# A two-level Strassen matmul with GELU: one more split product, two lent result buffers, and 21 buffer cells chosen anew

## The chip, the cores and the metric

The kernel runs on one core of a Trainium2 chip. The metric is device time in microseconds (us) of one execution. TensorE (PE) multiplies, VectorE (DVE), ScalarE (ACT) and GpSimd (POOL) work on tiles, and SyncE (SP) and POOL issue the transfers: here POOL fetches and SP stores.

## The reference

Two float32 matrices of 4096 x 4096 are multiplied, and the tanh form of GELU is applied to the product:

```python
def reference(a, b):
    x = np.matmul(a, b)
    return 0.5 * x * (1 + np.tanh(np.sqrt(2 / np.pi) * (x + 0.044715 * x**3)))
```

## The kernel before

**Two levels of Strassen.** A, B and C are cut into quadrants of 2048 x 2048 (called "11", "12", "21", "22"). Instead of eight products of quadrants the kernel computes seven, P1 to P7, of sums of quadrants (the Winograd form: P1 is A11 x B11, P2 A12 x B21, and P3 to P7 use sums on one or both sides), and adds them up into the four quadrants of C. Operands are 16-bit floats, sums of products are 32-bit.

The work is tiled by **groups**: a group is one block of 512 rows and 512 columns in each of the four quadrants of C, so there are 4 x 4 = 16 groups. One product of a group is 512 x 2048 x 512: four row tiles (i = 0 to 3) by 16 steps of 128 x 512 columns, 64 matmuls, over four banks of PSUM (`acc`). Such a product can itself be **split**: seven smaller products of half its size instead of eight. Done on one group (`split`, `stage`, `part_pe` at L1011; its matmuls are L1026), it takes 14 parts of eight matmuls of 256 columns; its operands are sums of A blocks and B blocks made by VectorE (`combine2`, L941), its parts are added in PSUM by VectorE (`add_part`, L1044) and copied by ScalarE (L1040).

The groups come in three kinds:

- group 0 (`first_group`), before anything is in place;
- groups 1 to 5 (`raw_group`), which work from the matrices themselves in the order P1, P2, P5, P6, P7, P4, P3, with unsplit matmuls at L581. The table `RAW_CUT` says which of their products are split. A split P7 runs in turns with P4; a split P3 runs in turns with P4 too, or, where P7 is split as well, is handed to the next group and runs in turns with its P1 (`pending`);
- groups 6 to 15 in five pairs of neighbouring column blocks (`late_pair`): (6,7), (8,9), and so on. Here a product is split over both blocks at once (`split_pair`), with matmuls of full 512 columns (L1853), 14 parts of eight: `ORDER = "10 11 70 71 20 21 60 61 50 51 30 31 40 41"`, the first digit is the small product and the second its row tile. B operands come back from DRAM in quarters (`k_unit`, one per product and column block, fetched at L822), and running sums are parked there (`park`).

In `split_pair` the operands are made in place as soon as the parts that read the old contents have been issued:

```python
                if once("T1", "1", "7"):
                    sums["5"] = inner_sum(1, as_inner(sums["6"]), x11, sums.get("7"))
...
                    make("12", "22", "11")
                if once("T4", "1", "2"):
                    make("21", "21", "11")
```

T1's two steps make what part 5 multiplies (a sum of A blocks, then one of B blocks of 128 x 4096), T4 makes part 4's B operand over the block that parts 20 and 21 read. Behind part 7 ScalarE copies its bank out (`copy_bank`, L1862); behind parts 1 and 6 it copies a bank into another (`copy_over`, L1865), which a later part then adds to.

**Results.** A finished bank is added by VectorE to a small buffer (`add_bank`, L1299) or from a buffer into a bank (`into_bank`, L1304), goes through GELU on ScalarE (L1277, or straight from PSUM) and is stored by SP (L822). Result buffers are called `y` in the profile and are 128 x 512 floats; they come out of the list `free_small`. Beside it, VectorE adds up squares of B (L1384), which a check of the value range uses.

**Cells.** Everything else in SBUF lies in 28 cells of 128 x 2048 16-bit values (`bR_73` to `bR_80`, `aD_81` to `aD_84`, `stage_85` and `stage_86`, each of which holds two). `free_cells` is the list of free ones; `new_cell` takes its first, `new_unit` and `new_chunk` neighbours of it. A cell taken early is one whose former readers have to be through before it may be written.

**Who sets the order.** The program is first built as a list of operations with what each reads and writes (`Plan.add`). `Plan.schedule` then walks through planned time: TensorE's operations keep their order, and each other engine takes, among those ready, the one that is due first. Durations and transfers are planned with fixed costs. So another cell or buffer changes what an operation must wait for, hence its planned start, hence the order written for VectorE, ScalarE, POOL and SP, in places far behind as well. The engines run that order as written.

Of the kernel before, what the change touches and what calls it, by code (L numbers as in the profile page):

```python
# [91 lines left out]
    return {name: mode for mode, names in kw.items() for name in names.split()}  # L92


N_RAW = 6
RAW_MAKES = {}
RAW_CUT = {1: "P3", 2: "P7 P3", 3: "P3", 4: "P3", 5: "P7"}
GROUPS = {
    6: modes_of(m="P1 P2 P3 P4 P5 P6 P7"),
    7: modes_of(m="P1 P2 P3 P4 P5 P6 P7"),  # L100
# [14 lines left out]
TURN_PLAN = (("11", "11", "P1", None), ("21", "12", "S4", None), ("12", "S1", "P5", None), ("22", "S2", "next", "P1"))  # L115
BEHIND = 2
FRONT = 2
LEND = ()
SQUARES_3 = ("12",)
NEAR = 2  # L120
CASTS = {4: ((1, 'P3'), (2, 'P3')), (8, 'P5'): ((0, 'P2'),)}
# [225 lines left out]
def half_path(  # L347
# [379 lines left out]
    for n, whats in (  # L727
# [20 lines left out]
        for what in whats.split():  # L748
# [11 lines left out]
            for h in (0, 1) if half else (None,):  # L760
# [9 lines left out]
                else:  # L770
                    pairs = [({"A": load_a, "B": load_b}[x], xs) for x, xs in args]
# [34 lines left out]
    free_cells, free_small = [], [x for x in (8, 9, 0, 1, 2, 3, 10, 11, 12, 13, 14) if x not in SPARE]  # L806
# [18 lines left out]
    def c(x):  # L825
        return ("c", x)

    def new_cell():
        return free_cells.pop(0)

    def new_unit():
        got = []
        for _ in range(2):
            pairs = [k for k, x in enumerate(free_cells) if x ^ 1 in free_cells[:k]]
            x = free_cells[pairs[0]] & ~1
            free_cells.remove(x)
            free_cells.remove(x + 1)
            got += [x, x + 1]
        return got

    def new_chunk():
        x = min((k for k in free_cells if k ^ 1 in free_cells), key=lambda k: max(map(free_cells.index, (k, k ^ 1)))) & ~1
        free_cells.remove(x)
        free_cells.remove(x + 1)
        return x
# [3 lines left out]
    def new_small(lend=False):  # L849
        own = [f for f in free_small if f in lent]  # L850
        if lend and own:
            free_small.remove(own[0])
            return own[0]
        if not free_small or lend and len(free_cells) > 1:
            x = new_cell()
            for h in range(2):
                f = len(small)
                small.append(cell(x)[:, h * W : (h + 1) * W].bitcast(F32))
                plan.alias["f", f] = ("c", x, h)
                free_small.append(f)  # L860
            lent[f], lent[f - 1] = (x, f - 1), (x, f)
            if lend:
                return free_small.pop()
        return free_small.pop(0)
# [57 lines left out]
    def a_quarter(src, q):  # L922
        if src[0] == "raw":
            t = a_phys[src[1], q // 2].rearrange("p x y -> p (x y)")
            return t[:, (q % 2) * CELL : (q % 2 + 1) * CELL], [("a", src[1], q // 2, h) for h in (0, 1)]
        x = src[1][q]
        return cell(x), [c(x)]
# [59 lines left out]
    def unsplit(*args):  # L987
        run(quarters(*args))

    def run(*lists):  # L990
        for row in zip(*lists):
            for fn in row:
                fn()
# [115 lines left out]
    def stages_of(z, done=None, ready=None):  # L1109
        z.ready = ready  # L1110

        def one(k):
            stage(z, k)
            if k == 4 and done and not ready:
                for i in range(RT):
                    done(i)

        return [lambda k=k: one(k) for k in (1, 2, 3, 4)]
# [16 lines left out]
    def made_here(unit_cells, release=lambda p: None, ends=lambda: None):  # L1135

        def quarter(kw):
            k, w = int(kw[0]) - 1, int(kw[1]) - 1
            x = unit_cells[2 * k]
            return wide_of(x)[:, :, w * HC : (w + 1) * HC], [("c", x, w), ("c", x + 1, w)]  # L1140

        def prepare(k):
            if k == 1:
                combine2(*quarter("11"), quarter("12"), quarter("11"), -1)
            elif k == 2:
                combine2(*quarter("11"), quarter("22"), quarter("11"), -1)
                combine2(*quarter("12"), quarter("22"), quarter("12"), -1)
            elif k == 3:
                combine2(*quarter("21"), quarter("21"), quarter("11"), -1)
                ends()  # L1150

        at = {"1": "11", "2": "21", "3": "22", "4": "21", "5": "11", "6": "11", "7": "12"}

        def of(p):
            t, toks = quarter(at[p])
            if p == "1":
                toks = toks + quarter("12")[1]
            full = wide_of(unit_cells[2 * (int(at[p][0]) - 1)])

            def rhs(j, wide):  # L1160
                return full[:, j, :] if wide else t[:, j, :]

            return rhs, toks, (lambda: release(p))

        return of, prepare
# [109 lines left out]
    def out_of(gi, i, ih, jh, f):  # L1275
        t = sm(f)
        act("gelu", lambda: nc.scalar.activation(t, t, ACT.Gelu_apprx_tanh), [("f", f)], [("f", f)])  # L1277
        store_out(gi, i, ih, jh, f)
# [17 lines left out]
    def add_bank(f, s, i, g=None):  # L1296

        g = f if g is None else g
        dve("add", lambda: nc.vector.tensor_tensor(out=sm(g), in0=bank(s, i), in1=sm(f), op=ALU.add),  # L1299
            [("f", f)], [("f", g), ("p", s, i)])  # L1300
        return g
# [110 lines left out]
    def raw(quad):  # L1412
        return ("raw", slots["a"][quad])

    def blk(cells):
        return ("blk", cells)

    def slot_cells(slot):
        return tuple(slot * 4 + q for q in range(QPH))
# [67 lines left out]
    def raw_group(gi, keep_units, makes, fetch=(), next_nb=None, turn=None, pending=None):  # L1487

        cut = RAW_CUT.get(gi, "").split()

        mb, nb = groups[gi]
        X, Y = 0, 1
        sl = dict(slots["b"])
        s11, s12, s21, s22 = (slot_cells(sl[x]) for x in ("11", "12", "21", "22"))
# [33 lines left out]
        if turn:  # L1528
            s2, s3 = SA, blk(SB)
        else:  # L1530
            s2, s3 = SB, raw("21")
# [84 lines left out]
        def load_next(quad, old):  # L1616
            if next_nb is not None:
                load_raw(next_nb, quad, sl[old])

        def here(cells):  # L1620
            return made_here(cells)

        def p4(s, fresh, done):
            return quarters(s, lambda q: a_quarter(raw("22"), q), lambda q: s21[q], fresh, done)
# [9 lines left out]
        def p7_out(i):  # L1634
            add_bank(u[i], X, i)
            out_of(gi, i, 1, 0, u[i])
            f = new_small(i in LEND)
            add_bank(v[i], X, i, f)
            out_of(gi, i, 1, 1, f)

        def p4_ends():
            if turn:
                turn_quad(turn, "22", raw("22"), (24, 26))
            if next_nb is None and gi + 1 in REFETCH:
                for q in range(QPH):
                    fetch_unit_to(nb, "P2", q, s21[q])
# [5 lines left out]
        if "P7" in cut:  # L1652
            def p4_add(i):
                add_bank(u[i], Y, i)

            if "P4" in cut:
                fourth = stages_of(split(Y, raw("22"), here(s21), True), p4_add)
            else:
                fourth = p4(Y, True, p4_add)
            if "P4" in cut:  # L1660
                run(fourth)
                run(stages_of(split(X, s3, here(s12), True), p7_out))
            else:
                run(fourth, stages_of(split(X, s3, here(s12), True), p7_out))
            load_next("21", "12")
            load_next("12", "21")
            p4_ends()
            if "P3" in cut:
                later_ = third, after
            else:  # L1670
                unsplit(Y, lambda q: a_quarter(blk(s2), q), lambda q: s22[q], True, c12)
                after()
        else:
            unsplit(X, lambda q: a_quarter(s3, q), lambda q: s12[q], False, u3)
            load_next("21", "12")
            if "P3" in cut:
                for i in range(RT):
                    add_bank(u[i], Y, i)
                if turn:
                    free_cells.extend(SB)  # L1680
                run(p4(X, False, p4_out), third())
                if turn:
                    for x in SB:
                        free_cells.remove(x)
                p4_ends()
                load_next("12", "21")
            else:
                run(p4(X, False, p4_out))
                p4_ends()
                load_next("12", "21")  # L1690
                unsplit(Y, lambda q: a_quarter(blk(s2), q), lambda q: s22[q], False, c12)
            after()
# [61 lines left out]
    def late_pair(ga, turn):  # L1754
# [29 lines left out]

        new = {}
        k = new_unit() if turn else None

        def new_a(now):
# [335 lines left out]
    with tc.manual_schedule():  # L2124
# [20 lines left out]
        temps.extend(TEMPS)  # L2145
        for gi in range(N_RAW, LAST, 2):
            if gi + 1 == LAST:
# [40 lines left out]
```

## Time and profile before

| what | value |
|---|---|
| three runs | 1446.91, 1448.10, 1448.36 us; median 1448.1 |
| the profiled execution | 1447.74 us, of which the span of the trace is 1446.1 |
| TensorE | 1435.4 us busy (99%), 6963 matmuls, full clock throughout |
| VectorE | 1212.2 us busy (84%) |
| ScalarE, GpSimd | 707.0 us (49%), 485.7 us (34%) |
| moved by DMA | 378.94 MB |

The table's engines overlap. "Busy" is a union of the instructions' times on one engine; PEld, where it is shown, is the loading of weights. A row of the timeline gives start, duration, engine, line, operation, output and inputs, the shape and a count of equal instructions in a row, and in brackets how long the engine had stood before it and what released it. In the chain of waits a row gives start, duration and what the end of the program hung on at that time. A row of the view of waits gives the sum, the number and the longest of a kind.

### The profile page before, as it was taken

What the parts mean: (1) busy time and instruction counts of PE and PEld (TensorE: products, weight loads), DVE (VectorE), ACT (ScalarE), POOL (GpSimd) and SP (SyncE); (2) the same over time, 40 slices, a digit from 0 to 9 for tenths busy, and PEclk for the clock granted to TensorE, in tenths of its full rate; (3) what the DMA queues carried; (4) which work ended last, traced back from release to release, by engine and by line L of the source; (5) the groups of instructions that cost most, each with busy time, mean ns of one, the idle gap of its engine ahead of it and who ended that gap; (6) DMA issues with size and microseconds to landing.
All of it is one profiled execution on the core that took longest, in us unless ns stands there. A gap on an engine that the chain in (4) does not pass through costs nothing.

```text
span 1446.1 us, 20123 instructions
## 1 busy us (share of the span) xinstructions
PE 1435.4 (99%) x6963; PEld 681.3 (47%) x6963; DVE 1212.2 (84%) x1315; ACT 707.0 (49%) x1480; POOL 485.7 (34%) x888
## 2 busy tenths in 40 slices
PE   9999999999999999999999999999999999999998
PEld 3444464564544645444444444444444444444443
DVE  2598988986877779989998989887998889887877
ACT  5656764365884543462655413453463623343133
POOL 8765251443244413331422342222322213111220
PEclk9999999999999999999999999999999999999999
DMA  9999999999999999998979899979898867775763
GB/s 172 197 222 238 300 272 265 256 275 258 235 241 235 267 281 235 283 294 284 311 283 316 270 310 316 286 220 342 226 350 251 299 232 258 279 276 195 276 249 127
DMA packets 205181, 378.94 MB, mean 262 GB/s; under 512 B 21008, under 2 KB 115728, under 8 KB 205072
## 3 DMA queue, kind: packets, MB, share of 16 engines
q0 software_dynamic: 146752, 245.42, 70.0%
q1 hardware_dynamic: 58320, 132.15, 24.4%
q8 instruction: 57, 0.93, 0.3%
q14 instruction: 52, 0.43, 0.1%
HBM read 333.45 MB, written 138.42 MB: 326 GB/s over the span
## 4 chain that ended last, share of the span: by engine, by line
PE 93%; DMA 3%; POOL 3%; issue 1%; DVE 1%; ACT 0%; DVEq 0%; POOLq 0%
PE acc L1853 58%; PE acc L581 30%; PE acc L1026 5%; POOL bR L485 2%; DMA stage<-in_a_dram 1%; POOL stage L485 1%; DMA bR<-in_b_dram 1%; DMA bR<-k_unit 0%; DVE y L1299 0%; DVE bR L941 0%; DVE y L1384 0%; DVE aD L566 0%; ACT y L1862 0%; POOL aD L485 0%; ACT stage L494 0%
## 5 line engine op out<-in xcount | busy, mean ns | idle before, releaser
L1853 PE MATMUL acc<-bR 128*128 128x512 f16 x1536 | 339.5, 379 | 1.7 <-DVE bR L941 1.2
L941 DVE TENSOR_TENSOR bR<-bR 128x2048 f16<-128x2048 f16 (+1 forms) x159 | 263.4, 1669 | 35.4 <-PE acc L1853 22.7
L822 POOL DMA_DIRECT2D bR<-k_unit x234 | 126.8, 544 | 492.0 <-PE acc L1853 355.9
L1853 PEld LDWEIGHTS <-bR 128*128 128x128 f16 x1776 | 173.8, 98 | 211.6 <-issue 2.3
L581 PE MATMUL acc<-bR,aT 128*128 128x512 f16 x1088 | 239.7, 379 | 0.9 <-DVE y L1299 0.9
L1853 PE MATMUL acc<-bR,aT 128*128 128x512 f16 x1008 | 223.6, 379 | 0.0
L1853 PEld LDWEIGHTS <-aT 128*128 128x128 f16 x1344 | 131.5, 98 | 158.6
L1865 ACT COPY acc<-acc 128x512 f32<-128x512 f32 x140 | 79.7, 570 | 245.9 <-PE acc L1853 229.3
L822 POOL DMA_DIRECT2D bR<-in_b_dram x256 | 138.3, 548 | 182.1 <-PE acc L581 61.2
L1299 DVE TENSOR_TENSOR y<-acc,y 128x512 f32<-128x512 f32 x251 | 165.6, 682 | 40.5 <-PE acc L1853 17.5
L581 PE MATMUL acc<-bR,aD 128*128 128x512 f16 x832 | 180.9, 379 | 0.0
L581 PEld LDWEIGHTS <-aT 128*128 128x128 f16 x1152 | 112.8, 98 | 132.2 <-issue 1.2
L1379 ACT ACTIVATE y<-bR 128x1024 bf16<-128x1024 f16 x128 | 130.6, 1051 | 69.8 <-DVE y L1384 62.5
L581 PEld LDWEIGHTS <-aD 128*128 128x128 f16 x928 | 90.6, 98 | 109.9 <-DVE aD L566 0.7
L1853 PE MATMUL acc<-bR,aD 128*128 128x512 f16 x624 | 138.4, 379 | 0.0
L1277 ACT ACTIVATE y<-y 128x512 f32<-128x512 f32 x160 | 98.4, 629 | 67.6 <-DVE y L1299 67.2
L1853 PEld LDWEIGHTS <-aD 128*128 128x128 f16 x784 | 76.7, 98 | 92.5
L1862 ACT COPY y<-acc 128x512 f32<-128x512 f32 x99 | 57.9, 586 | 94.6 <-PE acc L1853 83.9
L1384 DVE TENSOR_TENSOR y<-y 128x1024 bf16<-128x1024 bf16 x120 | 82.2, 686 | 23.2 <-ACT y L1379 21.8
L458 DVE STREAM_TRANSPOSE aT<-stage 128x1024 uint32<-128x1024 uint32 (+2 forms) x42 | 52.3, 1274 | 33.1 <-DMA stage<-in_a_dram 30.9
L1853 PE MATMUL acc<-stage,aT 128*128 128x512 f16 x336 | 75.6, 379 | 0.0
L1304 DVE TENSOR_TENSOR acc<-acc,y 128x512 f32<-128x512 f32 x100 | 67.9, 690 | 2.1 <-ACT acc L1865 1.1
(124 smaller groups left out, 1645.8 us busy)
## 6 DMA issues: line engine op xcount, KB each, us to landing
bR<-k_unit POOLq DMA_DIRECT2D x234, 512.0 KB, 7.5
out_dram<-y SPq DMA_DIRECT2D x204, 256.0 KB, 7.0
bR<-in_b_dram POOLq DMA_DIRECT2D x352, 128.0 KB, 6.0
k_unit<-bR SPq DMA_DIRECT2D x76, 512.0 KB, 6.2
stage<-in_a_dram POOLq DMA_DIRECT2D x92, 256.0 KB, 9.7
stage<-k_unit POOLq DMA_DIRECT2D x46, 512.0 KB, 7.9
k_unit<-stage SPq DMA_DIRECT2D x28, 512.0 KB, 5.3
out_dram<-bR SPq DMA_DIRECT2D x46, 256.0 KB, 7.4
```

Source lines behind the costliest of these rows:

```text
L581: nc.tensor.matmul(acc, sa[:, j // 2, i * P : (i + 1) * P, j % 2], sb[:, j, :], start=start and j == 0, stop=stop and j == 3, skip_group_c ...
L822: return plan.add(queue, COST[queue], lambda: eng.dma_start(out=dst, in_=src), r=r, w=w, size=MOVE[what] * SPREAD, weight=weight, **kw)
L941: nc.vector.tensor_tensor(out=dst, in0=xa, in1=ya, op=ALU.add if op > 0 else ALU.subtract)
L1026: nc.tensor.matmul(PS[s][i][:, :] if wide else PS[s][i][:, w * HC : (w + 1) * HC], sa[:, j // 2, r * P : (r + 1) * P, j % 2], rhs(j, wide) ...
L1277: act("gelu", lambda: nc.scalar.activation(t, t, ACT.Gelu_apprx_tanh), [("f", f)], [("f", f)])
L1299: dve("add", lambda: nc.vector.tensor_tensor(out=sm(g), in0=bank(s, i), in1=sm(f), op=ALU.add), [("f", f)], [("f", g), ("p", s, i)])
L1304: dve("add", lambda: nc.vector.tensor_tensor(out=bank(s, i), in0=bank(s, i), in1=sm(f), op=ALU.add), [("f", f)], [("p", s, i)])
L1379: act("square", lambda t=t, src=src: nc.scalar.activation(t, src, ACT.Square), [c(cx)], [("f", f)], slack=60.0)
L1384: dve("add16", lambda t=t, u=u: nc.vector.tensor_tensor(out=u, in0=u, in1=t, op=ALU.add), [("f", f)], [("f", e)], slack=60.0)
L1853: nc.tensor.matmul(bank(w, i), sa[:, jx // 2, r * P : (r + 1) * P, jx % 2], bv[:, jx, :], start=p in "17" and jx == 0, stop=jx == NJ - 1, ...
L1862: act("copy", lambda: nc.scalar.copy(out=sm(f), in_=bank(w, i)), [("p", w, i)], [("f", f)])
L1865: act("copy", lambda: nc.scalar.copy(out=bank(*dst), in_=bank(*x)), [("p", *x)], [("p", *dst)])
```

## The change

Two tables are changed; a third is added with the code that reads it:

```diff
+CHOICE = {
+    2: 4, 6: 2, 11: 2, 12: 2, 14: 4, 29: 2, 42: 3, 50: 1, 59: 3, 71: 2, 73: 2, 75: 1,
+    77: 1, 78: 2, 83: 1, 85: 2, 86: 1, 90: 3, 93: 2, 187: 1, 188: 1,
+}
-RAW_CUT = {1: "P3", 2: "P7 P3", 3: "P3", 4: "P3", 5: "P7"}
+RAW_CUT = {1: "P3", 2: "P7 P3", 3: "P3", 4: "P7 P3", 5: "P7"}
...
-LEND = ()
+LEND = (2, 3)
...
+    taken = [0]
+
+    def choice(n):
+        taken[0] += 1
+        return min(CHOICE.get(taken[0], 0), n - 1)
+
     def new_cell():
-        return free_cells.pop(0)
+        return free_cells.pop(choice(len(free_cells)))
...
-            x = free_cells[pairs[0]] & ~1
+            x = free_cells[pairs[choice(len(pairs))]] & ~1
...
     def new_chunk():
-        x = min((k for k in free_cells if k ^ 1 in free_cells), key=lambda k: max(map(free_cells.index, (k, k ^ 1)))) & ~1
+        pairs = [k for k, x in enumerate(free_cells) if x ^ 1 in free_cells[:k]]
+        x = free_cells[pairs[choice(len(pairs))]] & ~1
```

`RAW_CUT`: group 4 splits P7 as well; its P4 and P7 run in turns, and its P3 goes to group 5's P1. `LEND`: in every raw group with a split P7 (2, 4 and 5), the last two results of C22 (i = 2 and 3, `p7_out`) are written into half of a free cell each, instead of into buffers of the `y` list:

```python
            f = new_small(i in LEND)
            add_bank(v[i], X, i, f)
            out_of(gi, i, 1, 1, f)
```

`CHOICE`: the allocations with these numbers take a later entry of the list of free cells. A branch for a case that no group has is removed. Lines behind the table move by 4 to 11: L581 becomes L585, L822 L826, L941 L952, L1026 L1037, L1299 L1310, L1384 L1395, L1853 L1860, L1862 L1869, L1865 L1872.

On TensorE only group 4 changes: 64 matmuls of 512 columns become 112 pieces, two of them of 512 columns and the rest of 256. VectorE gets 20 operations more for it: four sums of A blocks (128 x 2048), four of B blocks (128 x 8 x 256), four adds of 128 x 256 in PSUM and eight adds of 128 x 512. On the other engines the order moves; three places follow.

VectorE, the end of group 2, where its split P7 and P4 end and group 3's P1 begins. `acc` are the banks, `y` the result buffers, rows with `y_92` are sums of squares. Before:

```order
L1299 TENSOR_TENSOR y_88<-acc_102,y_100 128x512
L1299 TENSOR_TENSOR y_90<-acc_104,y_90 128x512
L1299 TENSOR_TENSOR y_96<-acc_103,y_89 128x512
L1299 TENSOR_TENSOR y_87<-acc_104,y_97 128x512
L1299 TENSOR_TENSOR y_98<-acc_105,y_98 128x512
L1384 TENSOR_TENSOR y_92<-y_92,y_94 128x1024
L1384 TENSOR_TENSOR y_92<-y_92,y_93 128x1024
L941 TENSOR_TENSOR bR_79<-bR_79 128x8x256
L1299 TENSOR_TENSOR y_99<-acc_105,y_95 128x512
```

After:

```order
L952 TENSOR_TENSOR stage_86<-aD_81,aD_82 128x2048
L1310 TENSOR_TENSOR y_88<-acc_102,y_100 128x512
L1310 TENSOR_TENSOR y_101<-acc_103,y_101 128x512
L1310 TENSOR_TENSOR y_96<-acc_103,y_89 128x512
L1310 TENSOR_TENSOR y_90<-acc_104,y_90 128x512
L1310 TENSOR_TENSOR y_98<-acc_105,y_98 128x512
L1310 TENSOR_TENSOR stage_86<-acc_104,y_97 128x512
L1310 TENSOR_TENSOR stage_85<-acc_105,y_95 128x512
L952 TENSOR_TENSOR bR_79<-bR_79 128x8x256
```

The last two results go into `stage` cells and stand together with the other adds; the two sums of squares and the sum of B blocks that stood ahead of the last one now stand behind it, and a sum of A blocks stands ahead of the series.

POOL, the fetches for P3 of pair (6,7): `k_unit_1061` and `k_unit_1062` are that product's B operands of the first and the second column block, in four quarters each. Before:

```order
L822 DMA bR_78<-k_unit_1062 128x2048
L822 DMA bR_75<-k_unit_1061 128x2048 x2
L822 DMA bR_76<-k_unit_1062 128x2048 x2
L822 DMA bR_77<-k_unit_1061 128x2048 x2
L822 DMA bR_78<-k_unit_1062 128x2048
L822 DMA bR_73<-k_unit_1053 128x2048
```

After:

```order
L826 DMA bR_75<-k_unit_1061 128x2048
L826 DMA bR_76<-k_unit_1062 128x2048 x2
L826 DMA bR_77<-k_unit_1062 128x2048 x2
L826 DMA bR_75<-k_unit_1061 128x2048
L826 DMA bR_78<-k_unit_1061 128x2048 x2
L826 DMA bR_73<-k_unit_1053 128x2048
```

Of the eight quarters, the second block's last one was the eighth and is now the fifth.

VectorE in P7 of the same pair. `bR_79<-bR_78,aT_67` is T1's sum of A blocks. Before:

```order
L941 TENSOR_TENSOR bR_78<-aT_68,bR_79 128x2048
L941 TENSOR_TENSOR bR_76<-bR_75,bR_76 128x4096
L1299 TENSOR_TENSOR y_91<-acc_106,y_98 128x512
L941 TENSOR_TENSOR bR_79<-bR_78,aT_67 128x2048
L941 TENSOR_TENSOR bR_75<-bR_73,bR_76 128x4096
L941 TENSOR_TENSOR bR_74<-bR_74,bR_76 128x4096
```

After:

```order
L952 TENSOR_TENSOR bR_78<-aT_68,bR_79 128x2048
L952 TENSOR_TENSOR bR_75<-bR_73,bR_75 128x4096
L1310 TENSOR_TENSOR y_91<-acc_106,y_90 128x512
L952 TENSOR_TENSOR bR_79<-bR_78,aT_67 128x2048
L1310 TENSOR_TENSOR bR_80<-acc_102,bR_80 128x512
L952 TENSOR_TENSOR bR_76<-bR_76,bR_75 128x4096
L952 TENSOR_TENSOR bR_73<-bR_77,bR_75 128x4096
```

The last two rows of each are T1's and T4's B operands: before T1's stood first, now T4's does.

In P7 of pair (8,9) SP's stores stand otherwise: before, results left in the order `y_100`, `bR_79` twice, `y_93`, `bR_80`, `y_95`, `y_89`; now `y_98`, `bR_79` twice, `y_95`, `y_93`, `bR_80`, `y_96`. ScalarE's copies of the banks behind parts 70 and 71 go into `y_93` and then `y_95`, in both.

More of the change, by code (lines that the diff above doesn't have):

```diff
@@ L1659, in raw_group @@
                 fourth = p4(Y, True, p4_add)
[L1660 to L1664, printed above, removed]
+            run(fourth, stages_of(split(X, s3, here(s12), True), p7_out))
             load_next("21", "12")
```

## Prediction

> **What bounds the kernel now.** The first view is the page's busy line, the second its row of granted clocks, the third its chain by engine.
>
> ```profile
> PE 1435.4 (99%) x6963; PEld 681.3 (47%) x6963; DVE 1212.2 (84%) x1315; ACT 707.0 (49%) x1480; POOL 485.7 (34%) x888
> ...
> PEclk9999999999999999999999999999999999999999
> ...
> PE 93%; DMA 3%; POOL 3%; issue 1%; DVE 1%; ACT 0%; DVEq 0%; POOLq 0%
> ```
>
> TensorE is the bound: 1435.4 of 1446.1 us, at the full clock, so only two things change the time: how many columns it streams, and how long it stands. The view of TensorE's waits names where it stands after the first group:
>
> ```profile
> PE acc L1853 <- DVE bR L941: 1.2, 1, 1.2
> PE acc L581 <- DVE y L1299: 0.9, 1, 0.9
> PE acc L1853 <- ACT acc L1865: 0.5, 1, 0.5
> ```
>
> Three stalls, once each. All other idle time of the other engines costs nothing. So I go through four places: the product that is split, and these three.
>
> **The split of P7 in group 4.** Group 5's split P7 is what group 4's becomes. Its rows in the chain of waits, between full products of P4 (x16, L581), and a full product behind them:
>
> ```profile
> 556.90 1.96 PE acc L1026 x16
> 558.87 3.45 PE acc L581 x16
> 562.32 3.49 PE acc L1026 x32
> ...
> 579.70 13.81 PE acc L581 x64
> ```
>
> A full matmul of 512 columns takes 3.45/16 = 0.2158 us, one of 256 columns 3.49/32 = 0.1091. The 64 full ones go (13.81 us); 16 + 96 pieces come, of which two are 512 wide: 1.96 + 3 x 3.49 = 12.43. **-1.38 us**, provided that weight loads stay hidden. PEld's 681.3 us over 6963 loads are 98 ns each, and they and PE's 1435.4 us make 2116.7 in a span of 1446.1: they lie beside the matmuls, and at 109 ns a piece is still longer than a load. The Trainium skill speaks against this split: "TensorE: Matmul & The Clock Gate", section "Part 3: Packing small matmuls — row/col tiling", says that a weight load runs beside matmuls only where it goes to other row groups than theirs, and here every operand fills all rows. By that rule the product would go from 64 x (216 + 98) ns = 20.1 us to 112 x (109 + 98) = 23.2, 3.1 more instead of 1.38 less. The trace differs: the measured pace of the pieces has no room for a load.
>
> What the split adds elsewhere: on VectorE four sums of A blocks, four of B blocks, four half-width adds and eight more adds of a result; ScalarE changes four copies and four GELUs for as many smaller ones. Prices of VectorE, and its load around group 4's end (columns of the windows: us, PE, PEld, DVE, ACT, POOL, clock, DMA share, GB/s):
>
> ```profile
> L941 DVE TENSOR_TENSOR bR<-bR 128x2048 f16<-128x2048 f16 x92 | 110.3, 1218 | 11.4 <-PE acc L581 8.8 <-PE acc L1026 1.6 <-DMA bR<-in_b_dram 0.9
> ...
> 286.52 1.42 DVE L1044 TENSOR_TENSOR acc<-acc,y 128x256 f32<-128x256 f32 x4
> ...
> 460.00:475.00 15.00, 15.00 (x71) 6.77 (x70) 7.48 (x12) 7.73 (x12) 9.47 (x18) 1.00 1.06 192
> 475.00:500.00 25.00, 25.00 (x172) 16.65 (x171) 20.38 (x26) 12.65 (x23) 12.09 (x23) 1.00 1.16 261
> 500.00:525.00 25.00, 25.00 (x117) 11.35 (x116) 15.90 (x18) 11.94 (x16) 10.07 (x19) 1.00 1.10 248
> 525.00:550.00 25.00, 25.00 (x117) 11.33 (x116) 22.31 (x22) 8.15 (x9) 0.00 (x0) 1.00 0.79 314
> ```
>
> 8 x 1.22 + 1.42 + 8 x 0.61 (the eight adds at 291.45, below, took 4.87) = 16.0 us. VectorE's idle from 460 to 550 is 7.52 + 4.62 + 9.10 + 2.69 = 23.9. It fits, with 7.9 left; I cost it at **nothing**. If that cover is gone it is the rival on the slower side. The P3 that group 4 did beside its P4 now runs beside group 5's P1, with the same matmuls: nothing.
>
> The lent cells and the 21 other cells add no instruction. What they change is who waits for which buffer, and so the order on VectorE, POOL and SyncE; this is priced where TensorE stood, and where the new order makes it stand.
>
> **First stall, end of group 2.** TensorE's rows, then VectorE's:
>
> ```profile
> 295.83 2.75 PE L581 MATMUL acc<-bR,aT 128*128 128x512 f16 x12
> 299.51 1.02 PE L581 MATMUL acc<-bR,aT 128*128 128x512 f16 x4 [0.92 <-DVE y L1299]
> ...
> 291.45 4.87 DVE L1299 TENSOR_TENSOR y<-acc,y 128x512 f32<-128x512 f32 x8 [0.38 <-PE acc L1026]
> 296.25 1.47 DVE L1384 TENSOR_TENSOR y<-y 128x1024 bf16<-128x1024 bf16 x2
> 297.64 1.22 DVE L941 TENSOR_TENSOR bR<-bR 128x2048 f16<-128x2048 f16 x1
> 298.77 0.68 DVE L1299 TENSOR_TENSOR y<-acc,y 128x512 f32<-128x512 f32 x1
> ```
>
> Twelve matmuls from 295.83 end at 298.42; the next starts at 299.51: a stall of 1.09 (the profile's 0.92 counts from a modelled end). The bank is read out by the add at 298.77, which stands behind two adds of squares and a sum. After the change that add writes into the lent cell and directly follows the other eight; the only work put ahead of it is one sum of A blocks. From 296.25: + 1.14 (a sum's pitch, 298.77 - 297.64 rounded up) + 0.68 = 298.07, 0.35 ahead of 298.42. **-1.09.** The bound above is that it stays, 0; below, no more than 1.09 is there. I take the gain, since the order of rows gives it.
>
> **Second stall, P3 of pair 6.** TensorE, then POOL, VectorE and the chain of waits:
>
> ```profile
> 686.59 7.07 PE L1853 MATMUL acc<-bR,aD 128*128 128x512 f16 x32
> 694.89 2.32 PE L1853 MATMUL acc<-bR 128*128 128x512 f16 x10 [1.23 <-DVE bR L941]
> ...
> 680.15 0.54 POOL L822 DMA_DIRECT2D bR<-k_unit  x1 [0.33 <-PE acc L1853]
> ...
> 687.06 1.07 POOL L822 DMA_DIRECT2D bR<-k_unit  x2 [2.92 <-PE acc L1853]
> ...
> 692.54 2.29 DVE L941 TENSOR_TENSOR bR<-bR 128x4096 f16<-128x4096 f16 x1 [0.27 <-DMA bR<-k_unit]
> ...
> 687.06 5.37 DMA bR<-k_unit
> ```
>
> TensorE was due at 686.59 + 32 x 0.2158 = 693.50: a stall of 1.39. The sum at 692.54 needs both halves of the second column block's P3 operand, and their last quarter was the eighth of eight fetches, issued at 687.06 when its cell came free, landed 5.37 later. In the changed order that operand's last quarter is the fifth; the fifth went out at 680.15, so it lands at about 685.5, where the sum has to begin by 693.50 - 2.35 = 691.15. What is fetched last instead is the first block's second half, due at part 20, four parts of 8 x 0.2158 later than 693.50, at 700.40; landing at 692.43 it has 8.0 us. **-1.39**, between 0 and that.
>
> **Third stall, P7 of pair 8.** TensorE, ScalarE, SyncE:
>
> ```profile
> 895.18 3.62 PE L1853 MATMUL acc<-bR 128*128 128x512 f16 x16
> 899.27 2.97 PE L1853 MATMUL acc<-bR 128*128 128x512 f16 x13 [0.47 <-ACT acc L1865]
> ...
> 894.32 0.59 ACT L1862 COPY y<-acc 128x512 f32<-128x512 f32 x1 [5.27 <-DMA out_dram<-y]
> 894.86 0.63 ACT L1277 ACTIVATE y<-y 128x512 f32<-128x512 f32 x1
> 898.14 0.59 ACT L1862 COPY y<-acc 128x512 f32<-128x512 f32 x1 [2.66 <-PE acc L1853]
> 898.63 1.08 ACT L1865 COPY acc<-acc 128x512 f32<-128x512 f32 x2
> ...
> 883.72 12.13 SPq L822 DMA_DIRECT2D out_dram<-y  x4
> ```
>
> Due at 898.63, started at 899.27: 0.64. The copy at 898.63 is the one waited for; ahead of it in ScalarE's queue stands the copy at 898.14 into y_95. The profile names TensorE as what that one waited for, but the bank it reads was finished by part 71, before 895.18 - 3.45 = 891.73. What came at 898 is, as I read it, the store that still read y_95: the sixth of a bunch, first of the four at 883.72. The copy at 894.32, into y_93, waited for the fourth; so stores land some (898.14 - 894.32)/2 = 1.91 apart. After, y_95 is fourth and y_93 fifth: both copies can be done with by 894.32 + 1.91 + 0.5 = 896.73, against the 897.50 that is needed. **-0.64**, down to 0 if the bunch as a whole is later.
>
> **A new wait, P7 of pair 6.**
>
> ```profile
> 725.97 4.26 PE L1853 MATMUL acc<-bR 128*128 128x512 f16 x19
> ...
> 724.01 4.48 DVE L941 TENSOR_TENSOR bR<-bR 128x4096 f16<-128x4096 f16 x2
> 729.62 1.23 DVE L941 TENSOR_TENSOR bR<-aT,bR 128x2048 f16<-128x2048 f16 x1 [0.42 <-PE acc L1853]
> ```
>
> At 724.01 VectorE makes part 50's operand (T1) and then part 40's (T4). T4 is written over what parts 20 and 21 read, so it must wait for part 21's end, at 725.97. In the changed order T4 stands ahead of T1. VectorE then starts 0.20 after 725.97 (as it did at 729.62, 0.20 after sixteen matmuls from 725.97 ended at 729.42), needs 4.48 for both, and 0.06 passes until TensorE starts: 730.71. TensorE is through with parts 60 and 61 at 729.42. **+1.29.** Queued behind are a sum for part 30, two parts on, and an add for part 40, four on; at 1.2 and 0.7 us both are in time. The bound below is 0.
>
> **Sum:** -1.38 - 1.09 - 1.39 - 0.64 + 1.29 = -3.21. The profiled execution took 1447.74, so 1444.53; the median shown is 0.36 above it: **1444.9 us**.
>
> **Rivals.**
> *The waits come back* as new ones nearby: buffers and cells behind group 2 nearly all take other places, and with TensorE ahead by some us each fetch and store has as much less lead. The three stalls, gone from where they were, return in sum at about their size (3.12), and only the split's gain is left, with the new wait or without: 1446.7 to 1448.0. For it speaks that margins such as 0.35 and 0.77 us are small; against it that three stalls in 1360 us are few, and that each had one nameable cause. 0.28.
> *The new wait does not come* (part 21 ends early enough, or TensorE is already held up shortly before): 1443.6. The order of rows speaks against it. 0.13.
> *VectorE becomes the bound* at the end of group 4, the slower side: 16.0 us added to 23.9 of idle holds only if the idle is at the right time. It decides when more than 7.9 us of it can't be used. If that of 460 to 475 (7.52, before most of the split's work is released) and of 500 to 525 (9.10, after group 5's operands are due) are both out of reach, 7.3 are left and TensorE stands 8.7: 1453.6. Against it: the operands of 500 to 525 are not due at once, and groups 2 and 5 carry the same split with a stall of 1.09 at most. 0.08.
> By the skill's rule on weight loads the sum is -3.21 + 1.38 + 3.1 = +1.27, 1449.4; the pace of 109 ns speaks against it. 0.01.
> That the change does not do what it says is excluded: the rows of the order show it.
>
> **How the numbers follow.** The forecast has 0.50; its own range, with the terms of 1.09 to 1.39 each open, is 1443.6 to 1446.2. About 0.2% (2.9 us) is what a measurement of this kernel can tell from no change, so faster is below 1445.2, which takes two thirds of the forecast's chance and the second rival: 0.33 + 0.13 = 0.46. Within: 0.17 + 0.28 + 0.01 = 0.46. Slower: 0.08. The range goes from 1443.3 to 1448.1, leaving out the slow side and the edges.
>
> **What would show it.** TensorE's busy time falls by about 1.4; its waits no longer name the three rows, but one of about 1.3 us for L952 in P7 of pair 6; around 299, 695 and 899 it has none. The forecast is wrong if TensorE's waits show a new row of more than 1 us anywhere else, above all between 470 and 560, or for a DMA behind pair 6.

## The result, and the profile after

| | before | after |
|---|---|---|
| median of 13 runs each, side by side | 1448.30 us | 1445.61 us |
| lowest, highest | 1446.91, 1449.43 | 1444.30, 1446.74 |
| the profiled execution, its span | 1447.74, 1446.1 | 1444.84, 1443.2 |

The ratio is 0.9981 with a 95% interval of 0.9974 to 0.9989, or 1.6 to 3.8 us less; by the medians it is 2.7 less, and the prediction was 3.2 less (1444.9 against 1448.1). The busy line of the changed kernel, and its TensorE waits (sum, number, longest) without those of the first 70 us:

```profile
PE 1433.2 (99%) x7011; PEld 685.9 (48%) x7011; DVE 1225.0 (85%) x1335; ACT 706.3 (49%) x1484; POOL 484.5 (34%) x888
...
PE acc L1860 <- ACT y L1869: 1.1, 1, 1.1
```

TensorE is 2.2 us less busy with 48 matmuls more. The split explains 1.38 of it; the rest is of the size by which executions with the same matmuls differ (1435.4 to 1436.2 us in before and in the three runs below that leave its order almost as it is). Of the three waits none is left, and one has come. The chain of waits shows group 4's split P7 (the first two lines, and P3's first pieces in the second), the last full product of group 5, and the piece behind the one break that is left:

```profile
465.66 3.49 PE acc L1037 x32
...
479.56 5.45 PE acc L1037 x48
...
577.00 13.81 PE acc L585 x64
...
726.62 711.58 PE acc L1860 x3296
```

The pieces run at 3.49/32 = 109 ns, as those of group 5 did; 5.45 is 3.49 for 32 of them and 1.96 for P3's first 16.

**The end of group 2**, TensorE and then VectorE:

```profile
295.58 3.62 PE L585 MATMUL acc<-bR,aT 128*128 128x512 f16 x16
299.03 1.91 PE L1037 MATMUL acc<-bR,aD 128*128 128x256 f16 x16
...
293.13 3.08 DVE L1310 TENSOR_TENSOR y<-acc,y 128x512 f32<-128x512 f32 x5
296.12 1.28 DVE L1310 TENSOR_TENSOR stage<-acc,y 128x512 f32<-128x512 f32 x2
```

All sixteen matmuls follow one another (295.58 + 3.45 = 299.03). The two adds into the lent cells end at 297.40; the last four matmuls, which need the second, start at 298.17.

**P3 of pair (6,7)**, TensorE, POOL, VectorE:

```profile
683.88 7.07 PE L1860 MATMUL acc<-bR,aD 128*128 128x512 f16 x32
690.79 3.62 PE L1860 MATMUL acc<-bR 128*128 128x512 f16 x16
...
677.01 1.07 POOL L826 DMA_DIRECT2D bR<-k_unit  x2 [12.85 <-PE acc L1860]
...
684.70 2.27 DVE L952 TENSOR_TENSOR bR<-bR 128x4096 f16<-128x4096 f16 x1
```

No gap here either (683.88 + 6.91 = 690.79). The make, which was at 692.54 and late, ends at 686.97, 3.8 us early: its last two quarters, the fourth and fifth fetch, went out at 677.01.

**P7 of pair (8,9)**, TensorE and ScalarE:

```profile
892.40 7.07 PE L1860 MATMUL acc<-bR 128*128 128x512 f16 x32
...
890.09 1.07 ACT L1869 COPY y<-acc 128x512 f32<-128x512 f32 x2 [3.83 <-DMA out_dram<-y]
```

The two copies wait for a store once and run at 890.1 and 890.6. The second is 1.8 us ahead of parts 60 and 61 (892.40); in before it ran 3.0 us behind their start (898.14 against 895.18).

**P7 of pair (6,7)**, the new wait, TensorE and VectorE:

```profile
721.87 3.62 PE L1860 MATMUL acc<-bR 128*128 128x512 f16 x16
726.62 7.08 PE L1860 MATMUL acc<-bR 128*128 128x512 f16 x32 [1.14 <-ACT y L1869]
...
722.07 4.49 DVE L952 TENSOR_TENSOR bR<-bR 128x4096 f16<-128x4096 f16 x2 [1.03 <-PE acc L1860]
```

VectorE stands until 722.07, 0.20 after part 21's end at 721.87, and makes T4 and T1; TensorE, due at 721.87 + 3.45 = 725.32, goes on at 726.62: 1.30 us. The profile names a ScalarE copy as what came last; the makes end at 726.56, where the first run below shows which of the two it is.

### The profile page after: what moved, and what is told of

Its sections match the earlier page's. It is cut to its first block, busy times and chain, and to the rows that moved or that the text cites. A ratio compares the mean times of both kernels' runs of the same rounds, so it can differ in the third digit from the quotient of the medians.

```text
span 1443.2 us, 20223 instructions
## 1 busy us (share of the span) xinstructions
PE 1433.2 (99%) x7011; PEld 685.9 (48%) x7011; DVE 1225.0 (85%) x1335; ACT 706.3 (49%) x1484; POOL 484.5 (34%) x888
## 4 chain that ended last, share of the span: by engine, by line
PE 99%; DMA 1%; issue 0%; POOL 0%; ACT 0%; DVE 0%; DVEq 0%; ACTq 0%; POOLq 0%
PE acc L1860 59%; PE acc L585 30%; PE acc L1037 6%; PE acc L629 4%; DMA stage<-in_a_dram 1%; POOL stage L489 0%; DVE aT L462 0%; ACT y L1869 0%; ACT y L2029 0%; DVEq L462 0%; ACT acc L1872 0%; ACTq L1869 0%; POOLq L2179 0%
## 5 line engine op out<-in xcount | busy, mean ns | idle before, releaser
L1860 PE MATMUL acc<-bR 128*128 128x512 f16 x1536 | 339.5, 379 | 1.1 <-ACT y L1869 1.1
L952 DVE TENSOR_TENSOR bR<-bR 128x2048 f16<-128x2048 f16 (+1 forms) x163 | 268.2, 1659 | 41.3 <-PE acc L1860 30.2
L826 POOL DMA_DIRECT2D bR<-k_unit x234 | 126.6, 543 | 442.1 <-PE acc L1860 323.1
L1860 PEld LDWEIGHTS <-bR 128*128 128x128 f16 x1776 | 173.7, 98 | 210.9 <-DVE bR L952 1.6
L585 PE MATMUL acc<-bR,aT 128*128 128x512 f16 x1024 | 226.2, 379 | 0.0
L1860 PE MATMUL acc<-bR,aT 128*128 128x512 f16 x1008 | 223.6, 379 | 0.0
L826 POOL DMA_DIRECT2D bR<-in_b_dram x256 | 137.9, 544 | 217.4 <-DVE bR L952 66.7
L1860 PEld LDWEIGHTS <-aT 128*128 128x128 f16 x1344 | 131.5, 98 | 158.6
L1872 ACT COPY acc<-acc 128x512 f32<-128x512 f32 x140 | 79.9, 571 | 233.7 <-PE acc L1860 229.0
L1310 DVE TENSOR_TENSOR y<-acc,y 128x512 f32<-128x512 f32 x253 | 167.5, 684 | 21.5 <-ACT y L1304 10.2
L585 PE MATMUL acc<-bR,aD 128*128 128x512 f16 x832 | 180.9, 379 | 0.0
L585 PEld LDWEIGHTS <-aT 128*128 128x128 f16 x1088 | 106.4, 98 | 123.0
L585 PEld LDWEIGHTS <-aD 128*128 128x128 f16 x928 | 90.8, 98 | 109.4 <-DVE aD L570 0.3
L1860 PE MATMUL acc<-bR,aD 128*128 128x512 f16 x624 | 138.4, 379 | 0.0
L1860 PEld LDWEIGHTS <-aD 128*128 128x128 f16 x784 | 76.7, 98 | 92.5
L1869 ACT COPY y<-acc 128x512 f32<-128x512 f32 x99 | 57.7, 585 | 96.9 <-PE acc L1860 84.8
L1395 DVE TENSOR_TENSOR y<-y 128x1024 bf16<-128x1024 bf16 x120 | 82.3, 688 | 16.3 <-ACT y L1390 14.5
L1860 PE MATMUL acc<-stage,aT 128*128 128x512 f16 x336 | 75.6, 379 | 0.0
```

Of the source, the lines that this page charges most:

```text
L585: nc.tensor.matmul(acc, sa[:, j // 2, i * P : (i + 1) * P, j % 2], sb[:, j, :], start=start and j == 0, stop=stop and j == 3, skip_group_c ...
L826: return plan.add(queue, COST[queue], lambda: eng.dma_start(out=dst, in_=src), r=r, w=w, size=MOVE[what] * SPREAD, weight=weight, **kw)
L952: nc.vector.tensor_tensor(out=dst, in0=xa, in1=ya, op=ALU.add if op > 0 else ALU.subtract)
L1395: dve("add16", lambda t=t, u=u: nc.vector.tensor_tensor(out=u, in0=u, in1=t, op=ALU.add), [("f", f)], [("f", e)], slack=60.0)
L1860: nc.tensor.matmul(bank(w, i), sa[:, jx // 2, r * P : (r + 1) * P, jx % 2], bv[:, jx, :], start=p in "17" and jx == 0, stop=jx == NJ - 1, ...
L1872: act("copy", lambda: nc.scalar.copy(out=bank(*dst), in_=bank(*x)), [("p", *x)], [("p", *dst)])
```

## Experiments

In all of them the times stand against runs of the kernel before on the same chip.

### One part alone

The split alone is the kernel before with one line changed, the lent buffers alone likewise, and the table of cells alone is the kernel after with both undone:

```diff
-RAW_CUT = {..., 4: "P3", 5: "P7"}
+RAW_CUT = {..., 4: "P7 P3", 5: "P7"}
```
```diff
-LEND = ()
+LEND = (2, 3)
```
```diff
 CHOICE = {2: 4, 6: 2, ...}
-RAW_CUT = {..., 4: "P7 P3", 5: "P7"}
+RAW_CUT = {..., 4: "P3", 5: "P7"}
-LEND = (2, 3)
+LEND = ()
```

The split alone: 

> Only group 4's split of P7, with the old buffers. My theory: TensorE's work falls by 1.38 us, but the split brings its own copy of the wait at the end of group 2, since the last result again lands in a buffer that is being stored: laid along this kernel's order, the durations of before give a new stall of 0.3 to 0.7 us at the end of group 4 (near 487), the old 1.09 near 299 stays, the one near 694 falls from 1.39 to 0.2 to 0.7, and one of about 0.6 comes near 826. Time about 1 us below before. Rival: the split is free of waits by itself and the lent buffers only matter to group 2: no stall between 460 and 560, time 1.4 us or more below before.

Measured: 1455.0 us against 1447.8, ratio 1.0051 (1.0036 to 1.0067): **7.2 us slower.** At group 4's end:

```profile
486.30 2.75 PE L581 MATMUL acc<-bR,aT 128*128 128x512 f16 x12
489.39 1.02 PE L581 MATMUL acc<-bR,aT 128*128 128x512 f16 x4 [0.34 <-DVE y L1299]
```

488.89 was due, so 0.50 is lost, the copy of group 2's wait that the theory asked for; the 1.09 near 299 is there as well. But the size of the whole was missed. TensorE waits 4.0 us for fetches:

```profile
PE acc L1853 <- DMA stage<-k_unit: 2.1, 1, 2.1
PE acc L1853 <- DMA bR<-k_unit: 1.9, 2, 1.6
```

I had laid durations of engines along the order, and no transfers. And behind the longest of these waits TensorE went on at a lower granted clock, which nothing in the expectation allowed for (a row of the timeline, then a window with the clock as third number from the end):

```profile
825.29 4.22 PE L1853 MATMUL acc<-stage,aT 128*128 128x512 f16 x12 [0.79 <-DVE y L1299]
...
825.00:827.50 2.50, 2.21 (x6) 0.81 (x6) 2.50 (x3) 0.93 (x2) 0.55 (x1) 0.50 1.13 309
```

The row behind these twelve matmuls starts at 829.35, so they took 4.06 us, where 12 x 0.2158 = 2.59 is their time at the full clock. The last section has the clock of the other runs.

The lent buffers alone: 

> Only the two lent result buffers (in groups 2 and 5, which split P7 in before already). My theory: the stall of 1.09 us near 299 goes, but the cells taken for it give VectorE another order: a stall of about 2.4 us in group 3's P5 (near 346), where B sums come later, about 2.5 more in pair (6,7) near 731, and the 1.39 near 694 stays. Time 3 to 5 us above before. Rival: the lent buffers act by themselves: 1.1 us below before, nothing new.

Measured: 1464.0 us, ratio 1.0105 (1.0079 to 1.0131): **16 us slower.** The wait near 299 is gone and the one of group 3's P5 is there, and again more came from fetches than I had:

```profile
PE acc L1853 <- DMA bR<-k_unit: 6.8, 3, 4.5
PE acc L581 <- DVE bR L941: 2.4, 1, 2.4
```

The table of cells alone: 

> Only the 21 other cells, without the split and without lent buffers. My theory: the numbers of the allocations mean other places once the split and the lent cells are missing, so the table does nothing by itself: the 1.09 near 299 stays, the stall at P3 of pair (6,7) near 694 grows from 1.39 to about 4, and one of about 1 comes near 778. Time 2 to 5 us above before. Rival: the table is what removes the second and third stall: 2.0 us below before.

Measured: 1463.9 us, ratio 1.0104 (1.0089 to 1.0119): **16 us slower**; TensorE waits 8.8 us for fetches in three places and 4.1 for L952 in two. The rival fell in all three runs: no part is a gain by itself.

### One part left out

The kernel after with `CHOICE = {}`: 

> The changed kernel with an empty table of cells: split of P7 in group 4 and lent buffers alone. Theory: the three parts were fitted to one another, and the table is what takes away the waits that the other two bring: a stall of about 2.4 us in group 3's P5 (near 346), about 1.4 near 490, and waits for fetches in the pairs behind, 5 to 15 us above before in all. Rival: the table is a small correction: within 1 us of after, 2 us below before.

Measured: 1462.5 us against 1448.4, ratio 1.0101 (1.0075 to 1.0128): 14 us slower. The two waits that were named, beside 3.7 us for L949 and 4.4 for fetches in the pairs:

```profile
PE acc L582 <- DVE bR L949: 2.5, 1, 2.5
...
PE acc L1034 <- DVE stage L949: 1.6, 1, 1.6
```

The kernel after with group 4's P7 unsplit: 

> The changed kernel without the split: lent buffers and table of cells alone. Theory: with the split away the allocations shift against the table's numbers, so waits come in the pairs (about 2.5 us near 730, more near 751, and for fetches): slower than before by 3 to 15 us, though the wait near 299 is gone. Rival: the parts add up: 1.38 above after, 1.3 below before.

Measured: 1474.3 us, ratio 1.0177 (1.0159 to 1.0195): 26 us slower, beyond what was expected. 16.2 us are waits for fetches from `k_unit`, one of them 10 us, near 795. The row of the chain that ends this one:

```profile
781.89 15.71 DMA bR<-k_unit
```

A fetch of 512 KB, issued when its cell came free, takes 15.71 us, beside fetches of A that POOL issued between the others. So the three parts are one change: the table takes away what the split and the lent cells bring, at the numbers of allocations that they make. The third kernel of this kind, after without the lent cells, was not run.

### The new wait of 1.30 us

The first run orders T4 behind T1 for the planner:

```diff
...
-                    make("12", "22", "11")
+                    first.append(make("12", "22", "11"))
                 if once("T4", "1", "2"):
-                    make("21", "21", "11")
+                    make("21", "21", "11", after=first if ga == 6 and name == "P7" else ())
...
```

> The changed kernel, with T4's make put behind T1's in P7 of pair (6,7). My theory: the wait of 1.30 us near 726 was the order of these two on VectorE alone, so it goes and nothing takes its place: TensorE without a wait after the first group, 1.3 us below after (1444.3 where after is 1445.6). Rival: T4, S4 and the adds behind come later and hold up part 30 or 40 instead, or the copy by ScalarE that the profile names is what is waited for: the same time as after, with a wait within 10 us of 726.

Measured: 1445.43 us against 1447.79, ratio 0.9983 (0.9974 to 0.9992), so **nothing against after.** The rival held. TensorE in this run, POOL, and a row of its chain:

```profile
733.60 3.62 PE L1861 MATMUL acc<-bR,aT 128*128 128x512 f16 x16
737.93 1.02 PE L1861 MATMUL acc<-bR,aT 128*128 128x512 f16 x4 [0.72 <-DMA bR<-k_unit]
739.20 2.75 PE L1861 MATMUL acc<-bR,aT 128*128 128x512 f16 x12 [0.24 <-DMA bR<-k_unit]
...
730.61 1.61 POOL L826 DMA_DIRECT2D bR<-k_unit  x3 [0.33 <-DVE bR L952]
...
731.15 8.01 DMA bR<-k_unit
```

There is no wait near 726 any more, so it was the order on VectorE and not the copy that the profile named. But the planner had put T4 two places further back, and the fetch into the block that T4 reads could go out at 730.61 only; TensorE stood 0.88 and 0.41 at P4's first parts, 1.29 in sum. To see whether that has to be, the second run exchanges the two makes (`swap` holds them) after the planning, so that nothing else moves:

```diff
         self.schedule()
+        x, y = self.swap
+        x.start, y.start = y.start, x.start
...
```

> The changed kernel with T4's and T1's makes of P7 in pair (6,7) exchanged on VectorE, and no other instruction of any engine moved. Theory: the wait of 1.30 us near 726 goes; since both makes now end some 1.3 us earlier against TensorE's parts than in the run before (where T4 was put two places further back), the fetch into the block that they read goes out in time too: no wait between 700 and 760, time 1.3 us below after. Rival: the fetch of P4's operand lands when it lands, and TensorE, 1.3 us ahead, stands at P4's first parts instead, as in the run before (0.9 and 0.4 near 737): the same time as after.

Measured: 1444.37 us against 1447.66, ratio 0.9977 (0.9968 to 0.9987). TensorE, VectorE, POOL:

```profile
722.88 10.52 PE L1863 MATMUL acc<-bR 128*128 128x512 f16 x48
733.24 7.07 PE L1863 MATMUL acc<-bR,aT 128*128 128x512 f16 x32
...
721.96 4.48 DVE L955 TENSOR_TENSOR bR<-bR 128x4096 f16<-128x4096 f16 x2
...
726.96 1.08 POOL L829 DMA_DIRECT2D bR<-k_unit  x2 [6.18 <-PE acc L1863]
```

No gap here, and the fetch goes out at 726.96. Behind 70 us the whole view has one wait of TensorE, 0.97 at 83.21 in group 1, where the profiled execution of before has 0.2 and that of after none; so the span of this one, 1442.8, is only 0.4 below after's. This is the fastest of the kernels here: 3.3 us below before by the medians, where after is 2.7 below in its own runs. The two intervals overlap; that the 1.30 is gone is shown by the trace, that the time is lower than after's only as far as these medians go.

### The two other causes, by leaving out one transfer

SP's operation 243 is the store that still reads `y_95`; the kernel before is run without it:

```diff
         self.schedule()
-        for o in sorted(self.ops, key=lambda o: (o.start, o.n)):
+        order = sorted(self.ops, key=lambda o: (o.start, o.n))
+        [o for o in order if o.eng == "SP"][243].fn = lambda: None
+        for o in order:
             o.fn()
```

> The kernel before without the one store of a result that still reads y_95 in P7 of pair (8,9) (that tile of 128 x 512 of the output is left out), every other instruction in its place. Theory: the copy into y_95 waited for that store, so it follows right behind the copy into y_93 and the GELU at about 895.5, and the stall of 0.64 near 899 is gone. Rival: it waited for TensorE, as the row of the profile says: copy at 898.1, stall 0.64.

Measured, ScalarE of that run:

```profile
893.01 0.59 ACT L1864 COPY y<-acc 128x512 f32<-128x512 f32 x1 [4.83 <-DMA out_dram<-y]
893.98 0.63 ACT L1279 ACTIVATE y<-y 128x512 f32<-128x512 f32 x1 [0.39 <-DVE y L1301]
894.52 0.57 ACT L1864 COPY y<-acc 128x512 f32<-128x512 f32 x1
```

The second copy follows right behind the GELU: it starts 0.2 us behind the start of parts 60 and 61 (894.31 in this run), in before 3.0 behind. It was the store. That TensorE has no wait there would not show it: in the two runs of before's order that follow, which leave this place as it is, the copy starts 2.5 and 2.3 us behind, and TensorE loses 0.14 us and nothing; in the first of them the profile, too, names a store for this copy. So the 0.64 is the size that this stall had in one execution.

The same with POOL's fetch 379, the last quarter: 

> The kernel before without the last fetch of the second block's P3 operand in pair (6,7) (a quarter of that operand keeps old values), every other instruction in its place. Theory: the make at 692.54 stands in VectorE's order behind adds that end at 692.27, so without the fetch it starts 0.27 us earlier only, and the stall falls from 1.39 to about 1.1; the rest is the order, which the planner chose because it knew the fetch to be late. Rival, as my prediction had it: the fetch alone makes the stall, and it goes.

Measured, TensorE and VectorE:

```profile
687.13 7.07 PE L1855 MATMUL acc<-bR,aD 128*128 128x512 f16 x32
695.06 3.18 PE L1855 MATMUL acc<-bR 128*128 128x512 f16 x14 [0.86 <-DVE bR L943]
...
691.52 1.29 DVE L1301 TENSOR_TENSOR y<-acc,y 128x512 f32<-128x512 f32 x2
692.73 2.28 DVE L943 TENSOR_TENSOR bR<-bR 128x4096 f16<-128x4096 f16 x1
```

Due at 694.04, started at 695.06: 1.02 of 1.39 stay without the fetch. VectorE's order holds them. The runs without the store and with the add moved, which have this fetch, stand 1.03 and 1.19 at the same place: the share of the order is steady, and that of the fetch is 0 to 0.4 from one execution to another.

### Order or buffer at the end of group 2

`first` is the add into `y_99`, `behind` the last of the other adds:

```diff
         self.schedule()
+        self.first.start = self.behind.start + 1e-6
...
```

> The kernel before with the last add of group 2 (into y_99) moved ahead of the two sums of squares and the sum of B blocks, right behind the other adds; nothing else moved, and no lent buffer. Theory of my prediction: the order alone made the stall, so the add runs at 296.3 and the 1.09 near 299 goes. Rival: the store that still reads y_99 (the first of six issued from 292.83, median 6.6 us to landing) lets it run at 298 to 298.7 only, so 0.5 to 1.1 stays, and only another buffer takes it away.

Measured, VectorE and TensorE:

```profile
291.13 4.87 DVE L1300 TENSOR_TENSOR y<-acc,y 128x512 f32<-128x512 f32 x8 [0.38 <-PE acc L1027]
298.06 0.69 DVE L1300 TENSOR_TENSOR y<-acc,y 128x512 f32<-128x512 f32 x1 [2.06 <-DMA out_dram<-y]
...
295.51 2.75 PE L582 MATMUL acc<-bR,aT 128*128 128x512 f16 x12
298.81 1.02 PE L582 MATMUL acc<-bR,aT 128*128 128x512 f16 x4 [0.54 <-DVE y L1300]
```

The add stands 2.06 us for the store, and 298.81 - 298.10 = 0.71 of the 1.09 stays; what was put behind it is late in its turn (TensorE waits 0.8, at 307.61, for a sum of B blocks that it did not wait for). At this place the order alone was worth 0.4, and with the late sum nothing is left of it; the rest of the 1.09 needs the other buffer, as the run with the lent buffers alone, which has no wait near 299, confirms.

### How near VectorE is to the bound

Four or eight reductions that nobody uses, put between VectorE's rows:

```diff
+                self.extra()
...
+        plan.extra = lambda: nc.vector.tensor_reduce(
+            out=junk[:, :], in_=zeros[:, 0:1].to_broadcast([P, KC]), axis=AX.X, op=ALU.add)
```

> The changed kernel with four extra reductions on VectorE (of constants, nobody uses them, some 1.1 us each), spread through group 4's split P7 from about 462 to 477; no other instruction moved. By my prediction's sum VectorE has 7.9 us of idle left from 460 to 550, so 4.4 us more cost nothing: no wait there. Rival: the idle that counts is what stands ahead of the next due operand, and the durations laid along this order leave about 2 us there: TensorE stands 2 to 3 us in all between 480 and 495, time as much above after.

> The same with eight of these reductions, the other four spread from about 482 to 495. By the sum of idle time, 8.8 us against 7.9 left: TensorE stands about 1 us, if it stands at all, and late in the stretch. Rival, by what stands ahead of the next due operand: 4 to 5 us in all, from 480 on.

Measured: spans of 1446.3 and 1448.7 us, where after has 1443.2. With four, TensorE at group 4's end:

```profile
483.79 2.12 PE L1044 MATMUL acc<-bR,aD 128*128 128x512 f16 x16
486.32 1.02 PE L592 MATMUL acc<-bR,aT 128*128 128x512 f16 x4 [0.41 <-DVE y L1317]
488.64 1.02 PE L592 MATMUL acc<-bR,aT 128*128 128x512 f16 x4 [1.30 <-DVE y L1317]
489.84 1.89 PE L592 MATMUL acc<-bR,aT 128*128 128x512 f16 x8 [0.17 <-DVE stage L1317]
491.56 1.91 PE L1044 MATMUL acc<-bR,aD 128*128 128x256 f16 x16
```

From 483.79 to 491.56 there is work for 1.96 + 3.45, and 7.77 go by: 2.36, and 0.5 more near 472. So 2.86 of the four reductions' 4.5 us come through. With eight, the same 2.86 and then one more stall of 1.66 that ends at 500.48: 4.52 of 9.1. The rival held in both.

## Why the prediction was right, step by step

- **The split of P7, -1.38.** Right: TensorE's last full product of group 5 starts 2.70 us earlier than before (577.00 against 579.70), which are 1.38, the 1.09 of group 2, and 0.26 by which the first groups were faster in this execution (its first split piece is at 189.47, before at 189.73; the sum of the three is 2.73). The prediction's list of three stalls left out a fourth wait of before, 0.2 us at 82.46 in group 1, which is part of these 0.26; it comes and goes between executions (0.7 in the run without the fetch, none in the run with the add moved). ScalarE's count, put at as many, rises by four (1484 against 1480), and its busy time does not (706.3 against 707.0). By the rule on weight loads of the Trainium skill ("TensorE: Matmul & The Clock Gate", "Part 3: Packing small matmuls — row/col tiling") the product would have become longer and the time 1449.4; 1445.6 was measured, and the trace does not agree with the rule, at 109 ns a piece. The same section also lets a load go ahead into a background weight buffer, which the prediction did not weigh; no run here shows whether that is what happens.
- **The end of group 2, -1.09.** Right in size, wrong in part of its reason. The prediction put it down to the order; the run with the add moved shows that order alone gives 0.4 and that the store of the old buffer held the rest. The change brings both the order and another buffer, so the term came out.
- **P3 of pair (6,7), -1.39.** Right in size, half right in its reason. The trace of before already showed only 0.27 us of idle ahead of the make, and the run without the fetch leaves 1.02: most of the wait was the place of the make in VectorE's order. The earlier fetch matters, as I read it, because it lets the planner put the make at 684.70; no run shows this by itself.
- **P7 of pair (8,9), -0.64.** Right in its reason, the store, as the run without it shows. The size is that of one execution: 0.14 and nothing in two others of the same order.
- **The new wait, +1.29.** Right: 1.30 at the named place, and gone when the two makes are exchanged. Where the makes stay apart, it comes back at the next fetch, which is the first rival of the prediction on a small scale.
- **VectorE's 16.0 us at nothing.** Right for this kernel, with too wide a margin: the step took all idle time from 460 to 550 as cover, 7.9 us of it left. The idle time of these windows fell by 15.6 us, so the 16.0 were right. In the changed kernel they have 8.4 us of idle (15.00 - 13.40, 25.00 - 23.25, 25.00 - 22.77 and 25.00 - 22.22 below), but four reductions of 1.14 cost 2.86: about 1.7 us were free ahead of the next due operand. The slower rival was nearer than its chance said.

```profile
460.00:475.00 15.00, 15.00 (x106) 10.13 (x104) 13.40 (x18) 9.37 (x15) 8.72 (x17) 1.00 1.14 218
475.00:500.00 25.00, 25.00 (x177) 17.07 (x175) 23.25 (x33) 12.70 (x22) 12.91 (x24) 1.00 1.11 228
500.00:525.00 25.00, 25.00 (x133) 12.90 (x132) 22.77 (x28) 15.28 (x21) 8.64 (x16) 1.00 1.13 284
525.00:550.00 25.00, 25.00 (x118) 11.34 (x116) 22.22 (x22) 4.84 (x7) 3.21 (x7) 1.00 0.83 317
```

- **The sum.** TensorE's end moved from 899.27 + 542.35 = 1441.62 (the row below, from the chain of waits of before) to 726.62 + 711.58 = 1438.20, 3.42 earlier: the 3.20 of these terms and the 0.26 of the first groups. The span fell by 2.9 only, since 5.0 us lie behind TensorE's end now and 4.5 did before.

```profile
899.27 542.35 PE acc L1853 x2512
```

- **What was luck.** Two of the five terms are sizes of one execution, 1.39 (elsewhere 1.02 to 1.19) and 0.64 (elsewhere 0 and 0.14). And the sum has no term for transfers that come late behind the new cells: its rival, that the waits come back, puts them at 3.12 us, where the parts alone and the kernels with one part left out lose 7 to 26. That none came late here is a fact of this table of cells, which the prediction did not work out.

What stays open is why exactly each part alone brings so many late fetches: their waits are shown, but which cell held up which fetch was followed in one place only (the 15.71 us near 782).

## What to carry to other kernels

Where TensorE is busy 99% of the time and a planner sets the order, lay the trace's durations along the new order and look for each operand's margin; a sum of idle time says little, since only what stands ahead of the next due operand counts. Count the transfers too, above all where a buffer comes free late: the forecasts of the single parts, which left them out, were wrong by 8 us and more, and 4.0, 6.8 and 8.8 us of waits for fetches stand in those runs. Each long wait can cost more than its length, since the granted clock was lower behind some of them. And judge an edit of a split, its buffers and its allocation as one: here each alone costs 7 to 16 us, and together they gain 2.7.

## What the runs showed of the hardware that was not expected

A fetch of 512 KB took 5.37 us to land near 687 of before, 8.01 near 731 in the run with T1 first, and 15.71 near 782 in the run without the split. The Trainium skill, "DMA: Bandwidth & Descriptors", section "Anatomy of one DMA — SWDGE (gpsimd) path", gives 2.0 us plus the bytes at 436 GB/s for one, an estimate of 3.2 us; the traces agree with it as a floor only: the three fetches had others beside them.

The time of a matmul is no constant. With the same matmuls TensorE is busy 1436.8 us in the run of the split alone and 1433.2 in after, and 1442.6 in the run of the table alone and 1435.4 in before. Behind some of the long waits its granted clock is lower: 0.50 from 825.0 to 827.5 in the first of these runs, 0.50 from 670.0 to 675.0 in the second, 0.50 from 790.0 to 797.5 in the run without the split. From busy time and granted clock of such windows I estimate that this cost 1.5 us in the run of the split alone and 5.2 in that of the table alone. After's wait of 1.30 us left the clock at 1.00, and so did one of 3.1 near 627 in the run without the split; these runs give no length of wait from which on it falls.
